# Stick-breaking attention: the scan in place, and a row buffer of its own for the sigmoid

## The chip, the cores and the metric

The kernel runs on one core of one Trainium2 chip. The metric is the device time of one execution in microseconds. Five engines work side by side, each through a list of instructions in a fixed order: TensorE (PE in the profile, its weight loads PEld), VectorE (DVE), ScalarE (ACT), GpSimd (POOL) and SyncE (SP), which issues the DMAs.

## What is computed

One layer of a decoder with 2048 tokens of 1024 channels, all in 32-bit floats. The normalised input is projected to 6144 columns; these feed eight heads of stick-breaking attention and four heads of differential attention, and both branches are gated, merged, projected and normalised again. The change concerns the first branch:

```python
# A[t,s] = beta_ts * prod_{s<j<t}(1-beta_tj), s<t strictly
z = jnp.einsum('bqhd,bkhd->bhqk', q_blk, k) * scale
neg_log_1m_beta = jnp.where(mask, jax.nn.softplus(z), 0.0)
suffix = lax.cumsum(neg_log_1m_beta, axis=3, reverse=True) - neg_log_1m_beta
a = jnp.where(mask, jnp.exp(jax.nn.log_sigmoid(z) - suffix), 0.0)
out = jnp.einsum('bhqk,bkhd->bqhd', a, v)
```

## The kernel before

The sequence is worked off in two halves of 1024 tokens. In each half come four pairs of stick-breaking heads (called heads below, `s00` to `s03` in the first half, `s10` to `s13` in the second), then four differential heads (`d..`), and at the end the output stage (`y`, `o`). While one head attends, the projections of the next head and some of the gate columns are put between its instructions on TensorE (line 177). Their weights arrive by DMA and are split into two parts on GpSimd (lines 136 and 137).

`sb_group` holds the attention of one head for 512 queries. It goes backwards over chunks of 512 keys, from the diagonal chunk (`kc == G`) to chunk 0: one or two chunks in the first half, three or four in the second. A head has two halves of its pair and two groups of queries, so 6 chunks in the first half and 14 in the second. Each chunk has four rows, `r` = 0 to 3, of 128 queries. A row passes through:

- two matmuls for the scores into a PSUM bank (`a_S`, lines 384 and 385; three banks),
- the sigmoid on ACT (line 402), which writes `b`; in the diagonal chunk GpSimd then masks 128 columns of it (line 405),
- `g = 1 - b` on GpSimd (line 406),
- the scan on VectorE (line 408), from the last key to the first: the running product with `g`, less `b`. Each step multiplies the state by `g` and takes `b` from it, so that the state is the running product of `1 - b`, less one. Its start value is the first column of the same row's result in the chunk before. The weights A are the differences of neighbours in this result `R`; the kernel forms these differences on the values instead.

Then `R` is transposed on TensorE in blocks of 128 (line 414, `a_T`, two banks), split into a high and a low part by ACT (line 421, `a_h`) and VectorE (line 422, `a_l`), and multiplied by the values into the accumulator (`a_O`, lines 425 and 426).

`b`, `g` and `R` lie in buffers of the tag `row`: eight of them, each 2 x 512 floats per partition. A row's `b` and `g` share one; the results of two rows share one. So a chunk takes four buffers for `b` and `g` and two for `R`. A `b`/`g` buffer is free when its scan has ended, an `R` buffer when the last transpose of the chunk and the next chunk's scans have read it. The differential heads use the same eight buffers for their rows.

The order on each engine is made when the program is built: a scheduler takes instructions by their place in the code, moved back by fixed offsets for the transposes' products (`LATER_AV`) and the projections (`LATER`), and by `pace_products`, which ties the projections to the score matmuls. It also decides which of the eight buffers a tile gets, and so which earlier reader an instruction has to wait for.

## Time and profile before

| | |
|---|---|
| median of three runs | 2284.68 us (2282.75 to 2286.26) |
| profiled execution, its own time | 2286.18 us |
| its span in the trace | 2284.5 us |
| TensorE (PE) busy | 2184.0 us, 96% |
| VectorE (DVE) busy | 1486.4 us, 65% |
| ScalarE (ACT) busy | 942.7 us, 41% |
| GpSimd (POOL) busy | 846.3 us, 37% |
| scans (line 408, 192 + 128 of the groups shown) | about 385 us of VectorE |
| idle of ACT ahead of the sigmoid, until a scan ended | 202.4 us |
| granted TensorE clock, mean | 0.99 |

The times of one execution stand in a trace of it: one entry for each instruction with engine, line, start and duration, and for each idle stretch the event that ended it. Matmuls overlap, so an engine that is "busy" 96% of the time need not stream 96% of the time. The chain of waits follows the work that ended last back from the end, at each step to what released it.

### The profile page before, as it was taken

Reading aid. Unit: us, or ns where it says so; the run is one execution under the profiler, and the core shown is the slowest. Engines: PE = TensorE matmul, PEld = TensorE weight load, DVE = VectorE, ACT = ScalarE, POOL = GpSimd, SP = SyncE. Lnnn points to the kernel's source line nnn. Section 1 sums busy time; section 2 is a strip of 40 time slices with the busy share of each in tenths; the row PEclk is TensorE's granted clock in tenths of the full one; section 3 lists DMA queues with packets and bytes.
Section 4 is the critical chain, followed back from the end, with each engine's and each line's share of the span. In section 5 each row is a group of like instructions: output and inputs, shape, how many; then the busy total and the mean of one; then the engine's idle time right before and its main releaser. Section 6 shows DMA issues by size and latency. Waiting matters only on the chain.

```text
span 2284.5 us, 33674 instructions
## 1 busy us (share of the span) xinstructions
PE 2184.0 (96%) x11712; PEld 1837.2 (80%) x11712; DVE 1486.4 (65%) x3424; ACT 942.7 (41%) x2004; POOL 846.3 (37%) x1142
## 2 busy tenths in 40 slices
PE   6999999999999999999999999999999998999998
PEld 5788888888888778777777777787888878899997
DVE  6546565467557568787887877777767778444434
ACT  4324344344434434444444445454444444222221
POOL 2546446433232265454544543232222324111110
PEclk9999999999999999999999999999999999999999
DMA  4332323332444221221121121232222424544442
GB/s 127 113 119 93 119 74 109 110 106 84 129 136 132 88 83 56 65 68 62 45 72 51 47 74 53 69 97 66 79 84 75 121 81 158 166 136 143 137 152 90
DMA packets 204890, 220.99 MB, mean 97 GB/s; under 512 B 18864, under 2 KB 149936, under 8 KB 204720
## 3 DMA queue, kind: packets, MB, share of 16 engines
q1 hardware_dynamic: 204720, 218.83, 30.8%
q8 instruction: 93, 1.52, 0.3%
q14 instruction: 77, 0.63, 0.1%
HBM read 134.89 MB, written 67.11 MB: 88 GB/s over the span
## 4 chain that ended last, share of the span: by engine, by line
PE 71%; DVE 12%; ACT 5%; POOL 4%; issue 4%; DMA 3%; SPq 0%; DVEq 0%; ACTq 0%; POOLq 0%
PE g L177 13%; PE o L678 7%; PE y L177 6%; DVE a_R L408 6%; PE f_O L550 4%; PE a_T L414 3%; PE f_S L384 2%; PE zd L177 2%; PE f_S L385 2%; PE f_T L535 2%; POOL a_b L406 2%; PE a_O L425 1%; PE a_S L384 1%; ACT a_b L402 1%; PE a_O L426 1%
## 5 line engine op out<-in xcount | busy, mean ns | idle before, releaser
L406 POOL TENSOR_SCALAR a_b<-a_b 128x512 f32<-128x512 f32 (+2 forms) x320 | 227.1, 714 | 231.4 <-ACT a_b L402 222.6
L408 DVE TENSOR_TENSOR_SCAN a_R<-a_b,a_R 128x512 f32<-128x512 f32 x192 | 261.4, 1368 | 68.8 <-POOL a_b L406 50.9
L402 ACT ACTIVATE a_b<-a_S 128x512 f32<-128x512 f32 (+2 forms) x320 | 166.6, 534 | 244.3 <-DVE a_R L408 202.4
L422 DVE TENSOR_TENSOR a_l<-a_T,a_h 128x512 fp32r<-128x512 f32 (+1 forms) x320 | 186.3, 599 | 83.2 <-ACT a_h L421 72.9
L421 ACT ACTIVATE a_h<-a_T 128x512 fp32r<-128x512 f32 (+1 forms) x320 | 166.3, 534 | 131.7 <-PE a_T L414 112.5
L678 PE MATMUL o<-wt,m 128*128 128x512 f32 x768 | 210.7, 392 | 2.6 <-POOL wt L136 2.1
L514 ACT ACTIVATE f_row<-f_row,f_mx 128x1024 f32<-128x1024 f32 (+4 forms) x192 | 171.2, 894 | 90.4 <-DVE f_mx L507 85.8
L177 PE MATMUL g<-hh,g_w_hi 128*128 128x512 f32 x512 | 202.7, 396 | 0.0
L177 PE MATMUL g<-hl,g_w_hi 128*128 128x512 f32 x512 | 202.6, 396 | 0.0
L177 PE MATMUL g<-hh,g_w_lo 128*128 128x512 f32 x512 | 202.3, 395 | 0.0
L177 PE MATMUL y<-u,woh 128*128 128x256 f32 x1024 | 201.2, 281 | 1.1 <-DMA u<-ul_dram 0.6
L501 DVE CUSTOM_DVE_ANT_0 f_row<-f_S,f_bm 128x512 f32<-128x512 f32 (+3 forms) x304 | 168.6, 572 | 46.7 <-PE f_S L385 27.8
L414 PE MATMUL a_T<-ident,a_R 128*128 128x128 f32 x1088 | 169.7, 274 | 12.8 <-DVE a_l L422 9.4
L414 PEld LDWEIGHTS a_T<-ident,a_R 128*128 128x128 f32 x1088 | 133.2, 141 | 49.5 <-DVE a_l L422 16.8
L177 PEld LDWEIGHTS y<-u,woh 128*128 128x128 f32 x1024 | 165.6, 189 | 6.0 <-DMA u<-ul_dram 1.7
L678 PEld LDWEIGHTS o<-wt,m 128*128 128x128 f32 x768 | 140.4, 188 | 31.2 <-POOL wt L136 2.6
L542 ACT ACTIVATE f_h<-f_T 128x512 fp32r<-128x512 f32 (+2 forms) x176 | 85.2, 495 | 169.9 <-PE f_O L550 93.4
L543 DVE TENSOR_TENSOR f_l<-f_T,f_h 128x512 fp32r<-128x512 f32 (+2 forms) x176 | 98.1, 564 | 83.7 <-ACT f_h L542 80.5
L408 DVE TENSOR_TENSOR_SCAN a_R<-a_b 128x128 f32<-128x128 f32 (+3 forms) x128 | 123.7, 969 | 42.9 <-POOL a_b L406 40.4
L177 PE MATMUL y<-u,wol 128*128 128x256 f32 x512 | 143.0, 280 | 0.0
L136 POOL TENSOR_SCALAR g_w_hi<-g_w_raw 128x512 fp32r<-128x512 f32 x64 | 43.8, 702 | 205.4 <-PE g L177 85.4
L177 PEld LDWEIGHTS g<-hh,g_w_lo 128*128 128x128 f32 x512 | 96.6, 189 | 19.2
(1333 smaller groups left out, 5643.8 us busy)
## 6 DMA issues: line engine op xcount, KB each, us to landing
g_w_raw<-in_w_in_dram SPq DMA_DIRECT2D x64, 256.0 KB, 3.1
g_dram<-g_s SPq DMA_DIRECT2D x64, 256.0 KB, 2.4
x<-in_x_dram SPq DMA_DIRECT2D x16, 512.0 KB, 5.2
u<-uh_dram SPq DMA_DIRECT2D x64, 128.0 KB, 2.9
u<-ul_dram SPq DMA_DIRECT2D x64, 128.0 KB, 3.3
xr<-in_x_dram SPq DMA_DIRECT2D x32, 256.0 KB, 3.4
out_dram<-xr SPq DMA_DIRECT2D x32, 256.0 KB, 2.9
zd_w_raw<-in_w_in_dram SPq DMA_DIRECT2D x16, 256.0 KB, 3.1
```

Of the source, the lines that this page charges most:

```text
L177: pace["fill"].append((nc.tensor.matmul(ps, a[:, c, :], b[c], start=n == 0, stop=n == last).ins, len(pace["att"])))
L402: nc.scalar.activation(b, ps[:, :w], AF.Sigmoid, scale=SCALE)
L406: nc.gpsimd.tensor_scalar(g, b, -1.0, 1.0, ALU.mult, ALU.add)
L408: nc.vector.tensor_tensor_scan(R[r // 2][:, r % 2, :w][:, ::-1], g[:, ::-1], b[:, ::-1], init, ALU.mult, ALU.subtract)
L414: mark("T", nc.tensor.transpose(pt[:, r * P:(r + 1) * P], R[r // 2][:, r % 2, j * P:(j + 1) * P], ident))
L421: nc.scalar.activation(hi[:, c0:], pt[:, c0:], AF.Copy)
L422: nc.vector.tensor_sub(lo[:, c0:], pt[:, c0:], hi[:, c0:].bitcast(F32))
L501: nc.vector.tensor_tensor_reduce(rows[m][(c0 + p0) // HALF][:, (c0 + p0) % HALF:(c0 + p0) % HALF + pw], pss[m][:, p0:p0 + pw], bias_, scal ...
L514: nc.scalar.activation(rows[m][k][:, :w], rows[m][k][:, :w], AF.Exp, bias=mxs[m][:, 7:8], accum_out=sums[k][m])
L543: nc.vector.tensor_sub(lo[:, cs], pt[:, cs], hi[:, cs].bitcast(F32))
L550: mark("O", nc.tensor.matmul(O, a, r[:, ms], start=j == 0 and e == 0, stop=j == i and e == 2))
L678: nc.tensor.matmul(ps, M[a][c][:, tb * P:(tb + 1) * P], wt[m][b][c], start=i == 0, stop=i == 3 * NC - 1)
```

## The change

The two results of a row pair and `g` of the same two rows now lie in one buffer: GpSimd writes `g` into the place of `R`, and the scan overwrites it there. `b` has buffers of its own, one for two rows. A chunk takes two buffers for `b` and two for `R`, all allocated at the head of the chunk.

```diff
--- before.py
+++ after.py
@@ -390,22 +390,22 @@
         O = psO.tile([P, CH], F32, name=f"{n}_O", tag="O")
         prev = None
         for kc in range(G, -1, -1):
-            R = [T([P, 2, CH], F32, f"{n}_R{kc}{k}", "row") for k in range(2)]
+
+            B, R = ([T([P, 2, CH], F32, f"{n}_{x}{kc}{k}", "row") for k in range(2)] for x in "bR")
             for r in range(4):
                 w = P * (r + 1) if kc == G else CH
                 ww = max(w, 256)
                 qs = slice(r * P, (r + 1) * P)
                 ps = psS.tile([P, CH], F32, name=f"{n}_S{kc}{r}", tag="S")
                 qk(ps, K, q, qs, kc * CH, ww)
-                bg_ = T([P, 2, CH], F32, f"{n}_b{kc}{r}", "row")
-                b, g = bg_[:, 0, :w], bg_[:, 1, :w]
+                b, g = (t[r // 2][:, r % 2, :w] for t in (B, R))
                 nc.scalar.activation(b, ps[:, :w], AF.Sigmoid, scale=SCALE)
                 if kc == G:
 
                     nc.gpsimd.affine_select(b[:, qs], b[:, qs], pattern=[[-1, P]], compare_op=ALU.is_gt, fill=0.0, base=0, channel_multiplier=1)
                 nc.gpsimd.tensor_scalar(g, b, -1.0, 1.0, ALU.mult, ALU.add)
                 init = 0.0 if kc == G else prev[r // 2][:, r % 2, 0:1]
-                nc.vector.tensor_tensor_scan(R[r // 2][:, r % 2, :w][:, ::-1], g[:, ::-1], b[:, ::-1], init, ALU.mult, ALU.subtract)
+                nc.vector.tensor_tensor_scan(g[:, ::-1], g[:, ::-1], b[:, ::-1], init, ALU.mult, ALU.subtract)
             prev = R
             for j in range(4):
                 r0 = j if kc == G else 0
```

The instructions are the same in number and shape. What moves is their order and what they wait for. The place shown is one head of the second half (`a1100`, head `s11`), its two full chunks `kc` = 1 and 0. Names end in a chunk and row number and a running number; `b12` is chunk 1, row 2 before the change, while after it `b11` is chunk 1, rows 2 and 3. In brackets stand the engines that an instruction waits for.

ACT before, sigmoids of chunk 1 and the first two of chunk 0, among the high parts of earlier chunks:

```order
L402 ACTIVATE a1100_b11_9951<-a1100_S11_9948 128x512 [waits DVE_49]
L421 ACTIVATE a1011_h11_9658<-a1011_T11_9653 128x512 [waits PE_49]
L402 ACTIVATE a1100_b12_9958<-a1100_S12_9955 128x512 [waits DVE_49,PE_49]
L275 ACTIVATE s12k_a_10023<-s12k_ps1_10128 64x512 [waits PE_49]
L421 ACTIVATE a1011_h12_9669<-a1011_T12_9664 128x512 [waits PE_49]
L421 ACTIVATE a1011_h13_9680<-a1011_T13_9675 128x512 [waits PE_49,Activation_49]
L402 ACTIVATE a1100_b13_9965<-a1100_S13_9962 128x512
L277 ACTIVATE s12k_b_10024<-s12k_ps1_10128 64x512 [waits DVE_49]
L402 ACTIVATE a1100_b00_10059<-a1100_S00_10056 128x512 [waits DVE_49]
L421 ACTIVATE a1011_h00_9768<-a1011_T00_9763 128x512 [waits DVE_49,PE_49]
L402 ACTIVATE a1100_b01_10066<-a1100_S01_10063 128x512 [waits DVE_49]
```

ACT after, the same place:

```order
L402 ACTIVATE a1100_b10_9861<-a1100_S10_9865 128x512
L402 ACTIVATE a1100_b10_9861<-a1100_S11_9871 128x512
L421 ACTIVATE a1011_h10_9573<-a1011_T10_9568 128x512 [waits DVE_49,PE_49]
L421 ACTIVATE a1011_h11_9584<-a1011_T11_9579 128x512 [waits DVE_49,PE_49]
L402 ACTIVATE a1100_b11_9862<-a1100_S12_9877 128x512 [waits DVE_49]
L402 ACTIVATE a1100_b11_9862<-a1100_S13_9883 128x512
L275 ACTIVATE s12k_a_9943<-s12k_ps1_10046 64x512 [waits PE_49]
L421 ACTIVATE a1011_h12_9595<-a1011_T12_9590 128x512 [waits PE_49,Activation_49]
L277 ACTIVATE s12k_b_9944<-s12k_ps1_10046 64x512 [waits DVE_49]
L421 ACTIVATE a1011_h13_9606<-a1011_T13_9601 128x512 [waits PE_49,Activation_49]
L402 ACTIVATE a1100_b00_9974<-a1100_S00_9978 128x512
```

The sigmoids now stand in pairs, and of four one waits for VectorE where three did.

POOL after, `1 - b` of the same two chunks with the split of a weight among them (before, each of them waited for ACT, and none of these but two for another engine):

```order
L406 TENSOR_SCALAR a1100_R10_9863<-a1100_b10_9861 128x512 [waits DVE_49,Activation_49]
L406 TENSOR_SCALAR a1100_R10_9863<-a1100_b10_9861 128x512 [waits Activation_49]
L136 TENSOR_SCALAR zd11_w_hi_10541<-zd11_w_raw0_10543 128x512 [waits DMAHW7_49,PE_49]
L136 TENSOR_SCALAR zd11_w_hi_10541<-zd11_w_raw1_10547 128x512 [waits DMAHW0_49]
L137 TENSOR_TENSOR zd11_w_lo_10542<-zd11_w_raw0_10543,zd11_w_hi_10541 128x512 [waits PE_49,Pool_49]
L137 TENSOR_TENSOR zd11_w_lo_10542<-zd11_w_raw1_10547,zd11_w_hi_10541 128x512 [waits Pool_49]
L406 TENSOR_SCALAR a1100_R11_9864<-a1100_b11_9862 128x512 [waits PE_49,Activation_49]
L406 TENSOR_SCALAR a1100_R11_9864<-a1100_b11_9862 128x512 [waits Activation_49]
L406 TENSOR_SCALAR a1100_R00_9976<-a1100_b00_9974 128x512 [waits DVE_49,Activation_49]
L406 TENSOR_SCALAR a1100_R00_9976<-a1100_b00_9974 128x512 [waits Activation_49]
L406 TENSOR_SCALAR a1100_R01_9977<-a1100_b01_9975 128x512 [waits PE_49,Activation_49]
```

The waits for a buffer that an earlier scan or transpose has to free have moved to the first `1 - b` of each pair.

## Rows read from the trace of the kernel before

**Rows 1.** Busy time by stretch: PE, PEld, DVE, ACT, POOL busy (count); PEclk, DMA, GB/s.

```profile
60.00:445.00 385.00, 382.32 (x1900) 318.67 (x1900) 211.15 (x322) 145.61 (x299) 202.38 (x300) 1.00 0.32 101
806.80:963.80 157.00, 149.84 (x753) 123.36 (x751) 117.28 (x147) 68.58 (x138) 88.48 (x117) 0.99 0.24 74
963.80:1395.00 431.20, 398.04 (x2019) 315.65 (x2018) 341.11 (x407) 204.99 (x404) 222.08 (x306) 0.99 0.19 59
```

**Rows 2.** The same stretches, transposes of line 414 alone: PE, PEld; PEclk, DMA, GB/s.

```profile
60.00:445.00 385.00, 45.11 (x285) 34.90 (x285) 1.00 0.32 101
806.80:963.80 157.00, 25.68 (x168) 20.39 (x167) 0.99 0.24 74
963.80:1395.00 431.20, 93.59 (x602) 73.49 (x601) 0.99 0.19 59
```

**Rows 3.** Chain of waits, full stretch of the first half: start us, us, what.

```profile
344.90 0.77 PE a_T L414 x7
...
346.83 3.44 PE s03q_ps L177 x15
```

**Rows 4.** Waits, TensorE, 60 to 445: us in total, times, longest us.

```profile
PE s00vps L352 <- DVE vcarry L348: 1.5, 1, 1.5
```

**Rows 5.** Waits, all engines, 963.8 to 1395.

```profile
POOL a_b L406 <- ACT a_b L402: 169.0, 92, 3.6
ACT a_b L402 <- DVE a_R L408: 165.4, 99, 4.6
DVE a_R L408 <- POOL a_b L406: 36.8, 51, 1.4
DVE a_l L422 <- ACT a_h L421: 33.5, 38, 1.8
```

**Rows 6.** Chain of waits, 1048 to 1056.

```profile
1048.43 1.63 DVE a_R L408
...
1050.08 0.61 ACT a_b L402
...
1050.76 1.49 POOL a_b L406
...
1052.27 1.30 DVE a_R L408
...
1053.59 0.60 ACT a_b L402
```

**Rows 7.** Timeline, same place: start us, us, engine, line; idle before and releaser.

```profile
1050.55 1.27 DVE L408 TENSOR_TENSOR_SCAN a_R<-a_b,a_R 128x512 f32<-128x512 f32 x1
...
1050.76 1.48 POOL L406 TENSOR_SCALAR a_b<-a_b 128x512 f32<-128x512 f32 x1 [1.78 <-ACT a_b L402]
...
1057.37 0.62 POOL L406 TENSOR_SCALAR a_b<-a_b 128x512 f32<-128x512 f32 x1 [2.48 <-ACT a_b L402]
```

**Rows 8.** Groups of VectorE, 963.8 to 1395: busy us, mean ns, idle us before.

```profile
L408 DVE TENSOR_TENSOR_SCAN a_R<-a_b,a_R 128x512 f32<-128x512 f32 x120 | 162.6, 1358 | 37.4 <-POOL a_b L406 26.8 <-PE a_T L414 7.7 <-POOL g_w_hi L136 1.1
L422 DVE TENSOR_TENSOR a_l<-a_T,a_h 128x512 fp32r<-128x512 f32 (+3 forms) x169 | 102.9, 619 | 34.0 <-ACT a_h L421 33.5
L408 DVE TENSOR_TENSOR_SCAN a_R<-a_b 128x384 f32<-128x384 f32 (+3 forms) x46 | 47.5, 1033 | 11.0 <-POOL a_b L406 10.0
```

**Rows 9.** Tile a_b, 963.8 to 1395: ns min/median/max, first and last start us.

```profile
L406 POOL TENSOR_SCALAR a_b<-a_b x166: 295/620/1514, 964.6 to 1390.0; 128x512 f32<-128x512 f32 x132, 128x384 f32<-128x384 f32 x12, 128x128 f32<-128x128 f32 x11, 128x256 f32<-128x256 f32 x11
L408 DVE TENSOR_TENSOR_SCAN a_R<-a_b,a_R x120: 1252/1284/2293, 968.5 to 1391.0; 128x512 f32<-128x512 f32 x120
L405 POOL TENSOR_SCALAR_AFFINE_SELECT a_b<-a_b x46: 282/293/1220, 964.2 to 1356.6; 128x128 f32<-128x128 f32 x46
```

**Rows 10.** Tile s12k_w_hi, a weight split: ns min/median/max, first and last start us.

```profile
L177 PE MATMUL s12k_ps<-hh,s12k_w_hi x16: 392/397/398, 941.8 to 972.3; 128*128 128x512 f32 x16
...
L137 POOL TENSOR_TENSOR s12k_w_lo<-s12k_w_raw,s12k_w_hi x2: 1298/1300/1303, 928.0 to 929.2; 128x512 fp32r<-128x512 f32 x2
```

**Rows 11.** Group of VectorE, whole span: busy us, mean ns, idle us before.

```profile
L521 DVE SCALAR_TENSOR_TENSOR f_row<-f_row,f_l,f_row 128x512 f32<-128x512 f32 x8 | 6.0, 746 | 0.0
```

## The prediction

> **What bounds the kernel now.** I read the busy time by stretch first [rows 1], then counted what TensorE has to stream in each stretch [rows 1 to 3], then asked who makes it wait [rows 4, 5], and last followed the chain through one of those waits [rows 6, 7]. The changed code runs in two stretches: the stick-breaking heads of the first half of the sequence (60 to 445 us) and those of the second half (807 to 1395 us).
>
> TensorE's busy share does not separate the stages, because pipelined matmuls overlap. What separates them is the time that its instructions need when they stand back to back. A 512-column matmul then takes 3.44/15 = 0.23 us and a 128-column transpose 0.77/7 = 0.11 us [rows 3]; narrower matmuls I scale by columns. By the code each head has 32 matmuls of 256 and 16 of 384 columns. First half, four heads: 1900 instructions, 285 of them transposes [rows 1, 2], so 1423 x 0.23 + 128 x 0.115 + 64 x 0.17 + 285 x 0.11 = 384 us of the 385. TensorE is full there, and its costliest wait in the whole stretch is 1.5 us [rows 4]. Head 0 of the second half: 753 with 168 transposes, so 537 x 0.23 + 32 x 0.115 + 16 x 0.17 + 168 x 0.11 = 148 of 157 us (95%). Heads 1 to 3: 2019 with 602 transposes, so 1273 x 0.23 + 96 x 0.115 + 48 x 0.17 + 602 x 0.11 = 378 of 431 us (88%). **There 53 us are missing**, and only there can this change pay.
>
> What fills the gap: in these 431 us ACT waits 165.4 us, in 99 pieces, ahead of the sigmoid for the scan; POOL waits 169.0 us for the sigmoid; VectorE waits 36.8 us for POOL and 33.5 us for `a_h`, which stands behind the sigmoids on ACT [rows 5]. TensorE takes its part of it from both: a score matmul needs a bank that a sigmoid has emptied, a transpose a finished scan and a bank that `a_l` has left. The chain shows the loop: scan 1.63, sigmoid 0.61, POOL 1.49, scan 1.30, sigmoid, with 0.02 to 0.07 us between them [rows 6]. A sigmoid starts only when the scan of the row before it has ended. This is a buffer, not data: nothing in the mathematics ties row k's sigmoid to row k-1's scan. The eight `row` buffers are mostly held by R tiles that still wait for their transposes, and in the built program one buffer is handed from row to row. One turn without collision is 1.28 + 0.02 + 0.60 + 0.07 + 0.62 + 0.03 = 2.62 us; the stretch gives 431.2/168 rows = 2.57 us. **The loop sets the pace of heads 1 to 3.**
>
> **The change part by part.** No arithmetic is added or removed: 320 sigmoids, 320 `1 - b`, 320 scans as before, with the same shapes.
>
> *Fewer buffers.* A key chunk took six `row` tiles (two R, four b/g); it takes four (two B, two R). The order shows what comes of it: where nearly each sigmoid of a chunk waited on VectorE, only the first of the second pair does, and POOL's first `1 - b` of each pair now waits for VectorE or TensorE instead, since it is the first to write R. By the built program's placement the B pair of rows 2 and 3 takes the buffer of the B pair of rows 0 and 1, the other B pair one that an R gave up; of the R pairs one in two takes the buffer of the B pair just scanned, the other an older R's.
>
> *The new loop*, for four full rows: the scans 4 x 1.284 = 5.14 [rows 9]; ahead of one pair sigmoid, `1 - b` and gaps, 0.60 + 0.62 + 0.14 = 1.36; ahead of the other `1 - b` alone, 0.62 + 0.07 = 0.69; and inside each pair the second `1 - b` meets the first scan. The trace has that meeting: alone the operation took 0.62 us, started 0.2 us after a scan it took 1.48 and ended 0.42 us after it [rows 7], so I add 0.45 twice. Sum 8.09 us, 2.02 a row instead of 2.57, or 3 x 56 x 2.02 = 340 us. VectorE's other work has to find room: `a_l` 102.9 us [rows 8] and some 28 us (341.1 busy [rows 1] less 162.6 + 47.5 + 102.9 [rows 8]). The four `a_l` of a chunk (4 x 0.62 = 2.5 us [rows 8]) fit the 2.95 us of gaps, and the order puts `a_l` and key work between the scan pairs; the 28 us come on top: 368 us. POOL and the scans exclude each other, so their sum bounds too: clean scans 132 x 1.284 + 34 x 0.7 = 193; `1 - b` 132 x 0.62 + 34 x 0.5 = 99; masks 46 x 0.293 = 13 [rows 9]; 15 weights, each two pieces of 1.30 [rows 10] and two of the kind of a `1 - b` (0.62), 58; some 8 for `us_ul` at 1.3. That is 371 us.
>
> So three limits lie close together: VectorE 368, the VectorE and POOL pair 371, TensorE 378. With limits so near none is reached. I take 95% of TensorE's, what head 0 does with the same loop and more matmuls to put into it: 378/0.95 = 398 us, **a gain of 33 us**; the bounds are 0 and 53.
>
> By the Trainium skill (SBUF — State Buffer, "SBUF: two separate sides") the read and write ports that VectorE and GpSimd share are an exclusive lock for a whole instruction, held by a VectorE operation with two SBUF inputs against a GpSimd one that reads SBUF. By that rule the blocked `1 - b` ends its whole 0.62 us after the scan, 0.65 with the gap stands twice in the loop, and a row takes (8.09 + 0.40)/4 = 2.12 us, 357 for the three heads instead of 340. The trace agrees that the two exclude each other, but with 0.42 after the scan [rows 7], so that I keep 0.45; under either TensorE's 378 comes first.
>
> *Head 0* loses 157 - 148 = 9 us, in part at the turn between the halves; I take 2 of the 9. *First half*: nothing to gain at 384 of 385 us. *Scan in place*: the nearest row that overwrites an input is the 128x512 of `f_row`, 0.746 us [rows 11], against 0.62 for a mean `a_l` [rows 8]; at most 0.13 us a scan, 21 us over 168 rows on an engine with 90 us idle (431.2 - 341.1), so 0 on the path. *Moved instructions elsewhere*: the scheduler renumbers everything, but the differential heads and the output stage keep their buffers: 0, with 3 us either way. *Wait added on POOL*: behind it stand the weight splits, which the projections need. The trace has them early: `s12k_w_lo` ended at 930.5 and its first matmul began at 941.8 [rows 10], so 11 us cover it.
>
> Sum: 33 + 2 = 35 us. The profiled execution took 2286.18 us (span 2284.5), 1.5 above the median of the runs; 2286.2 - 35 = 2251, less 1.5: **2250 us**.
>
> **Rivals.** *The limits collide more* (gain 8 to 20, 2265 to 2277): scans in pairs, with POOL held under each, leave `a_l` late and TensorE's transposes wait. For it: 368, 371 and 378 are near each other, and the scans already average 1.358 us against 1.284 clean [rows 8, 9]. Against: the new loop's gaps match the `a_l` almost exactly. *TensorE reaches its limit* (378 us as in the first half: gain 53 + 5, 2227). Against: there VectorE is busy 211 of 385 us, here it would be 341 of 378 [rows 1]. *The change doesn't do what it says* (2280 to 2289): the freed buffers are swallowed by R tiles, which now are taken at `1 - b` instead of at the scan, about 2 us earlier, and wait for the same transposes; sigmoids then still go one by one. Against: the placement and the order's waits. *Slower*: POOL's `1 - b` waits for transposes of a chunk that TensorE has queued behind projections whose weights are still to be split on POOL. A block decides from 11.3 us; a chunk lasts 431.2/42 = 10.3 us, so a buffer that comes two chunks late (20.5) makes a projection 9.2 us late. Four such among the 15 weights eat 37 us, the whole gain; eight give 74 - 35 = 39 us more than before, 2323. For it: POOL works in order, and a wait for the buffer of R now stands on it. Against: those R tiles were transposed chunks earlier in the order.
>
> **How the numbers follow.** Forecast, 2237 to 2265: 0.60. Limits collide, 2265 to 2280: 0.16. TensorE's limit, below 2237: 0.08. No effect: 0.06. Slower: 0.10. The range leaves out the last two and a tip at either end: 2232 to 2277. What a measurement of this kernel can tell from no change is about 0.2%, 4.6 us: faster 0.84, within 0.06, slower 0.10.
>
> **What would show it.** Right: heads 1 to 3 take about 398 us instead of 431; ACT's wait for the scan ahead of the sigmoid falls from 165 us to under 60, VectorE's for `1 - b` from 37 to under 20; the first half stays at 385. POOL gains waits for VectorE and TensorE that cost nobody. Wrong in its size: VectorE over 90% busy there and TensorE still at 88 to 91%. Wrong in kind: projections that wait for weight splits, scans longer than 1.284 us where POOL is idle, or a first half beyond 390 us.

## The result

The change makes the kernel slower: 2338.53 us (median of four runs, 2333.7 to 2341.84) against 2284.1 of the kernel before on the same chip, ratio 1.0236 with the interval 1.0214 to 1.0257. The prediction was 2250.

The profiled execution has a span of 2332.0 us, 47.5 more than before. In the first half I take the start of a head as its first score matmul; in the second half as its first score against keys of the first half (tiles `s10k` to `s13k` and `d10k`), which in the stick-breaking heads comes 7 to 16 us behind the scores of the diagonal chunk. Starts are rounded, so the differences hold to 1 us. Counted so, the heads took (us):

| | before | after |
|---|---|---|
| four stick-breaking heads, first half | 394 | 398 |
| differential heads, first half | 369 | 369 |
| `s10` | 157 | 156 |
| `s11`, `s12`, `s13` | 143, 146, 134 (422 in all) | 156, 159, 144 (459) |
| first differential head, second half | 124 | 134 |
| the rest | 817 | 816 |

Counted from the first score of all, heads 1 to 3 took 433 us before and 467 after, `s10` 155 and 157. The loss lies in heads 1 to 3 of the second half, where the gain was expected, and ten more stand in the differential head behind them, in which their last chunks end. Engines and groups of the page after, with busy time, share and count, and for a group the mean in ns and the idle time ahead of it:

```profile
PE 2193.9 (94%) x11712; PEld 1841.5 (79%) x11712; DVE 1492.7 (64%) x3424; ACT 939.7 (40%) x2004; POOL 834.7 (36%) x1142
...
L408 DVE TENSOR_TENSOR_SCAN a_R<-a_R,a_R,a_b 128x512 f32<-128x512 f32 x192 | 272.3, 1444 | 35.0 <-POOL a_R L406 34.6
L406 POOL TENSOR_SCALAR a_R<-a_b 128x512 f32<-128x512 f32 (+2 forms) x320 | 202.9, 648 | 252.7 <-PE a_T L414 117.7
...
L402 ACT ACTIVATE a_b<-a_S 128x512 f32<-128x512 f32 (+2 forms) x320 | 157.1, 535 | 208.7 <-DVE a_R L408 150.7
```

No engine has much more to do. GpSimd's `1 - b` even got shorter (mean 648 ns, 714 before), and its idle time ahead of that line now ends with TensorE: 117.7 us wait for a transpose. By stretch (as [rows 1]; the last row is heads 1 to 3):

```profile
60.00:445.00 385.00, 378.35 (x1878) 314.98 (x1877) 207.50 (x311) 143.49 (x293) 208.94 (x294) 1.00 0.31 99
809.00:965.00 156.00, 148.21 (x728) 121.23 (x727) 112.65 (x138) 65.28 (x132) 83.80 (x109) 0.98 0.25 75
965.00:1424.00 459.00, 400.37 (x1983) 315.91 (x1982) 337.66 (x402) 197.46 (x396) 196.31 (x303) 0.98 0.17 53
```

The same heads before, 422 us of the 431 of [rows 1]:

```profile
964.00:1386.00 422.00, 389.04 (x1970) 308.40 (x1969) 333.33 (x399) 200.68 (x397) 215.63 (x299) 0.99 0.19 59
```

TensorE stands idle 59 us of the stretch, 33 before (its length less PE busy), and is busy 11 us longer, of which the granted clock explains up to 7 (last section). VectorE is busy 338 us (333 before), in a stretch that is 37 us longer: 74% instead of 79%. The waits in heads 1 to 3 after (us in total, times, longest), to be held against [rows 5]:

```profile
ACT a_b L402 <- DVE a_R L408: 113.0, 36, 5.5
POOL a_R L406 <- PE a_T L414: 102.2, 16, 9.8
ACT a_h L421 <- PE a_T L414: 82.2, 46, 4.3
POOL a_R L406 <- DVE a_R L408: 75.6, 34, 3.1
DVE a_l L422 <- ACT a_h L421: 70.0, 48, 4.1
...
PE a_S L384 <- ACT a_b L402: 35.5, 29, 2.5
DVE a_R L408 <- POOL a_R L406: 28.9, 48, 2.2
```

and of the same 422 us before:

```profile
ACT a_b L402 <- DVE a_R L408: 162.8, 98, 4.6
...
ACT a_h L421 <- PE a_T L414: 28.0, 31, 1.7
...
PE a_S L384 <- ACT a_b L402: 19.5, 26, 2.1
```

ACT's wait for the scan fell from 163 to 113 us, in 36 pieces instead of 98, so longer ones. New is the second line: sixteen times, 6.4 us on average, GpSimd stands before a `1 - b` until TensorE has transposed an old R. ACT's wait for transposes grew from 28 to 82 us, VectorE's for `a_h` from 32 to 70, TensorE's for the sigmoid from 20 to 36.

One of the sixteen, in order. In TensorE's order of the built program stand (names with their numbers; lines between left out)

```
L384 MATMUL a1111_S22_10886<-s11k_b_8512,s11q_1_1_1_9778 128x512
...
L384 MATMUL a1111_S23_10892<-s11k_b_8512,s11q_1_1_1_9778 128x512
...
L177 MATMUL s13k_ps0_11377<-hh_1_0_7857,s13k_w_hi_11365 128x512
...
L414 MATMUL a1110_T12_10631<-ident_78,a1110_R10_10583 128x128 x2
...
L414 MATMUL a1110_T13_10642<-ident_78,a1110_R11_10584 128x128 x2
```

`S22` and `S23` are the scores of rows 2 and 3 of a chunk. The results of both, `a1111_R21`, take the buffer of `a1110_R10`, whose last transposes (in `T12` and `T13`) come behind twelve projection matmuls of `s13k`. TensorE on the chip:

```profile
1084.91 0.39 PE L384 MATMUL a_S<-s11k_b,s11q 128*128 128x512 f32 x1
...
1088.61 0.39 PE L384 MATMUL a_S<-s11k_b,s11q 128*128 128x512 f32 x1
...
1096.35 0.40 PE L177 MATMUL s13k_ps<-hh,s13k_w_hi 128*128 128x512 f32 x1
...
1099.11 1.04 PE L414 MATMUL a_T<-ident,a_R 128*128 128x128 f32 x8
```

and the other engines (idle time before an instruction and what ended it in brackets):

```profile
1092.61 1.09 ACT L402 ACTIVATE a_b<-a_S 128x512 f32<-128x512 f32 x2 [1.81 <-DVE a_R L408]
...
1100.09 1.20 POOL L406 TENSOR_SCALAR a_R<-a_b 128x512 f32<-128x512 f32 x2 [9.81 <-PE a_T L414]
...
1100.45 0.69 DVE L422 TENSOR_TENSOR a_l<-a_T,a_h 128x512 fp32r<-128x512 f32 x1 [4.09 <-ACT a_h L421]
1101.06 1.30 DVE L408 TENSOR_TENSOR_SCAN a_R<-a_R,a_R,a_b 128x512 f32<-128x512 f32 x1
```

The two sigmoids had written b by 1093.7. Their `1 - b` could start only at 1100.09, when the transposes had read the old R; VectorE had nothing for 4.09 us and then got two scans at once. TensorE itself hardly paused here: it worked off projections that nobody waited for, ahead of transposes that everybody waited for. It pays later, when scores need banks that sigmoids have not emptied.

### The profile page after: what moved, and what is told of

It reads as the page before. It is cut to its first block, busy times and chain, and to the rows that moved or that the text cites. A ratio compares the mean times of both kernels' runs of the same rounds, so it can differ in the third digit from the quotient of the medians.

```text
span 2332.0 us, 33651 instructions
## 1 busy us (share of the span) xinstructions
PE 2193.9 (94%) x11712; PEld 1841.5 (79%) x11712; DVE 1492.7 (64%) x3424; ACT 939.7 (40%) x2004; POOL 834.7 (36%) x1142
## 5 line engine op out<-in xcount | busy, mean ns | idle before, releaser
L408 DVE TENSOR_TENSOR_SCAN a_R<-a_R,a_R,a_b 128x512 f32<-128x512 f32 x192 | 272.3, 1444 | 35.0 <-POOL a_R L406 34.6
L406 POOL TENSOR_SCALAR a_R<-a_b 128x512 f32<-128x512 f32 (+2 forms) x320 | 202.9, 648 | 252.7 <-PE a_T L414 117.7
L402 ACT ACTIVATE a_b<-a_S 128x512 f32<-128x512 f32 (+2 forms) x320 | 157.1, 535 | 208.7 <-DVE a_R L408 150.7
L408 DVE TENSOR_TENSOR_SCAN a_R<-a_R,a_b 128x128 f32<-128x128 f32 (+3 forms) x128 | 110.5, 883 | 35.8 <-POOL a_R L406 33.1
```

What stands on the lines that cost most here:

```text
L402: nc.scalar.activation(b, ps[:, :w], AF.Sigmoid, scale=SCALE)
L406: nc.gpsimd.tensor_scalar(g, b, -1.0, 1.0, ALU.mult, ALU.add)
L408: nc.vector.tensor_tensor_scan(g[:, ::-1], g[:, ::-1], b[:, ::-1], init, ALU.mult, ALU.subtract)
```

## The experiments

Two measures are used below, for heads 1 to 3 of the second half. Their time, counted as in the table above, is read from the traces. **Lead** is read from the built program: the TensorE work (0.23 us for 512 columns, 0.11 for a transpose, as [rows 3]) by which the first score of a row pair (for `b`, of its row) stands ahead of the last transpose that reads the old R in the buffer that this R or `b` takes, a mean over the tiles that take an R's buffer. In the example it reaches from `S22` to `T13`.

I began with two theories. **A**: `1 - b` takes R some 2 us earlier than the scan did, and so waits for transposes. **B**: buffers of `b` are released by pairs, after two scans, so sigmoids go in pairs and the three score banks run dry.

**Pairs without the scan in place.** `b` and `g` in pairs, R a buffer of its own, taken by the scan.

```diff
-            B, R = ([T([P, 2, CH], F32, f"{n}_{x}{kc}{k}", "row") for k in range(2)] for x in "bR")
+            B, Gt, R = ([T([P, 2, CH], F32, f"{n}_{x}{kc}{k}", "row") for k in range(2)] for x in "bgR")
```

> b and g each get buffers for two rows, but the scan writes into R buffers of its own: six tiles a chunk as before, in pairs, and R is claimed by the scan and not by 1 - b. Theory A (the change is slow because 1 - b now claims R and so stands behind the transposes that free it): R is claimed late again, the time falls back to within 15 us of before, 2270 to 2300, and POOL's wait for TensorE ahead of line 406 falls from 118 us to under 30. Theory B (the change is slow because b is freed for two rows at once, after two scans): as slow as the change or slower, 2325 to 2360, with ACT's wait for the scan at 110 us or more in heads 1 to 3.

2333.02 us (ratio 1.0222, 1.0199 to 1.0244): as slow as the change, without the early R. Against A.

**In place with a `b` for each row.** R is taken early as in the change, `b` as before.

```diff
-                b, g = (t[r // 2][:, r % 2, :w] for t in (B, R))
+                b, g = T([P, 2, CH], F32, f"{n}_b{kc}{r}", "row")[:, 0, :w], R[r // 2][:, r % 2, :w]
```

> The scan writes over 1 - b in place, but b has a buffer for each row (half of it unused), so b is freed after one scan. Theory A: slower than before all the same, since 1 - b still claims R: 2315 to 2360, with POOL waiting for TensorE ahead of line 406 for over 80 us. Theory B: back at before, 2275 to 2295, and POOL waits for TensorE under 30 us.

2302.03 us (1.0086, 1.0071 to 1.0101), heads 1 to 3 427 us: nearer to B's range than to A's, and 7 us above it. Some 20 of the 54 us stay with the early R; most goes with the pairs. It looked like B.

**A ninth buffer**, for the change and for the kernel before, with the memory taken from `Tl` and `zs`. That slows the end of the run by some 64 us in both (from the start of the last differential head 575 and 572 us against 510), so the four heads are what is read.

```diff
-    BUFS = {"K": 6, "V": 6, "Q": 8, "row": 8, "Th": 2, "Tl": 3, "vt": 1, "dv": 1, "zs": 2, "u": 2, "bm": 1, "bd": 1}
+    BUFS = {"K": 6, "V": 6, "Q": 8, "row": 9, "Th": 2, "Tl": 2, "vt": 1, "dv": 1, "zs": 1, "u": 2, "bm": 1, "bd": 1}
```

> The change with nine row buffers in place of eight; the room comes from one zs and one Tl buffer less. By the placement R then takes the buffer of an R from 4 chunks before instead of 3, while b pairs are still handed on inside a chunk. Theory A: the loop through TensorE's transposes is broken, POOL's wait for TensorE ahead of line 406 falls under 30 us, heads 1 to 3 fall from 467 us to 400 to 425, and the whole to 2255 to 2290 unless the two lost buffers cost more. Theory B: the b pairs are handed on as in the change, so 2325 to 2345.

> Control: the kernel before with the same nine row buffers and the same two buffers less. Theory A: its b/g buffer is still handed from row to row, so the loop of scan, sigmoid and 1 - b stays: 2275 to 2290. Theory B: the same, since it has no pairs. If the lost zs and Tl buffers cost much, it shows here: over 2290.

The change took 2411.69 us (1.0567, 1.0551 to 1.0583), the kernel before 2341.95 (1.0266, 1.0249 to 1.0283). The four heads of the change went from 615 to 637 us, those of before from 579 to 573. GpSimd's wait for transposes in the change did not shrink:

```profile
POOL a_R L406 <- PE a_T L414: 135.0, 22, 8.9
```

It was 102.2 in 16. The scheduler spent the buffer on running scores further ahead: in TensorE's built order the first transpose of a chunk now stands 31 us of work behind the chunk's last score instead of 27. The Trainium skill (Perfetto Trace Analysis, "Optimization Strategy") says that a gap which repeats on the engine that should be saturated can mean too little SBUF for the next tile. The trace has such gaps on TensorE, 59 us in heads 1 to 3 of the change, but with one buffer more they were larger, 71 us of 481.

**`b` kept for a head pair.** The change's eight buffers; the two of `b` are taken once and written again row by row, so that a row's half is free after its own scan (the last line stands in `sb_attend`; its passing on is left out).

```diff
-            B, R = ([T([P, 2, CH], F32, f"{n}_{x}{kc}{k}", "row") for k in range(2)] for x in "bR")
+            R = [T([P, 2, CH], F32, f"{n}_R{kc}{k}", "row") for k in range(2)]
+        B = [T([P, 2, CH], F32, f"b{hf}{p}{k}", "row") for k in range(2)]
```

> The change, but the two b buffers of a head pair are taken once for the whole head pair and written again chunk after chunk, instead of being taken anew for each chunk. The same eight buffers, the scan in place and R taken at 1 - b as in the change; what differs is the release: a row's half of b is free as soon as that row's own scan of the chunk before has read it, not when both scans of the pair have. Theory B (the pair's release makes sigmoids go in pairs, the score banks run dry and everything on TensorE behind them is bunched): the four heads of the second half fall from 615 us to 570 to 592, as in the kernel before (579), the run takes 2270 to 2300. Theory A (1 - b takes R early and waits for transposes, which is still so here): they stay at 605 to 625 us, the run at 2325 to 2350.

2339.59 us (1.0244, 1.0225 to 1.0263), the four heads 615 us. These are A's numbers, but A stands against the run without the scan in place. B falls: the release by pairs is gone, ACT waits 108 times for short scans instead of 36 times, and nothing is gained.

```profile
POOL a_R L406 <- PE a_T L414: 125.5, 24, 10.6
ACT b L402 <- DVE a_R L408: 115.8, 108, 3.5
```

**The same on the kernel before**, with four `b`/`g` buffers kept (taken in `sb_attend`) and so four for R.

```diff
-                bg_ = T([P, 2, CH], F32, f"{n}_b{kc}{r}", "row")
+                bg_ = BG[r]
+        BG = [T([P, 2, CH], F32, f"b{hf}{p}{k}", "row") for k in range(4)]
```

> The kernel before, with four b/g buffers taken once for a head pair, each written again by the same row of the next chunk, and so four left for R, two chunks deep. R is taken at the scan as before. Theory B: no sigmoid waits for the scan of the row ahead of it any more, ACT's wait for the scan in heads 1 to 3 of the second half falls from 163 us to under 60, and the run takes 2255 to 2285. A third theory, C (what counts is how far TensorE's transposes may stay behind the scores: R buffers that hold three chunks are needed): scans wait for transposes, the four heads take over 600 us instead of 579, the run 2300 to 2345. Theory A has nothing against this kernel and gives 2255 to 2285 as well.

2337.87 us (1.024, 1.0223 to 1.0257). The kernel before, with R taken late and no row waiting for the row ahead of it, is as slow as the change, which is against A. It is what theory C of this expectation had given. But with `b` kept above R had six buffers, three chunks deep, and that kernel was as slow, so the depth alone isn't it. ACT's wait for the scan halved, and scans now wait for transposes:

```profile
ACT b L402 <- DVE a_R L408: 83.2, 110, 1.8
...
DVE a_R L408 <- PE a_T L414: 34.8, 26, 3.9
```

**`1 - b` on ACT.** The kernel before without GpSimd in the loop, but for the mask of `g` in the diagonal chunk, whose two lines are left out here.

```diff
-                nc.gpsimd.tensor_scalar(g, b, -1.0, 1.0, ALU.mult, ALU.add)
+                nc.scalar.activation(g, ps[:, :w], AF.Sigmoid, scale=-SCALE)
```

> The kernel before, with 1 - b made on ACT as the sigmoid of the negated score instead of on POOL, so that a row needs two ACT instructions and its scan meets no 1 - b on VectorE's port (the masked block of a diagonal row is set on POOL for both). If the row-to-row loop through one b/g buffer sets the pace, a turn is 1.28 + 0.60 + 0.60 + 0.07 = 2.55 us against 2.57 measured: no change, 2272 to 2295. If the meeting of scan and 1 - b is what costs (scans mean 1.358 us against 1.284 clean, and 1 - b up to 1.48 instead of 0.62), heads 1 to 3 gain 12 to 30 us: 2250 to 2272. If ACT, with 0.6 us more for each of 320 rows, becomes the bound somewhere: above 2295.

2285.92 us (1.0004, 0.9995 to 1.0014). Without the meeting of scan and `1 - b` nothing is gained, unless ACT's added 0.60 us a row ate it, which this run cannot tell. Of the loop it says nothing, since the loop with ACT in GpSimd's place gave the same time. The exclusive port that the Trainium skill states (SBUF — State Buffer, "SBUF: two separate sides") agrees in kind with the 1.48 us of a blocked `1 - b` [rows 7]; that one ended 0.42 us after the scan, though, where the rule leaves it its whole 0.62.

What the slow kernels had in common was TensorE's order: the scores stood in clumps (15 to 19 spaces over 4 us between two scores, 3 to 9 in the quick ones). Theory **D**: the order costs. So I changed the order, and in the code nothing else; the scheduler then hands the eight buffers out anew.

**The change and the kernel before, scores tied to transposes.** In the second half the score of row r may not stand ahead of the transposes j = r of the chunk three before. The tie sets the order when the program is built; on the chip it adds no wait. `lastT` collects the last transpose of each bank `j` (lines between left out). In the views of these kernels the added lines move the sigmoid to line 406, `1 - b` to 410, the scan to 412 and the transposes to 418.

```diff
+                lastT.append(tr.ins)
-                qk(ps, K, q, qs, kc * CH, ww)
+                first = qk(ps, K, q, qs, kc * CH, ww)
+                if hf and len(lastT) >= 12:
+                    tc.add_manual_dep(first, lastT[r - 12].name, mybir.DependencyInfo(mybir.DependencyClass.NoSync, mybir.DependencyReason.DATA), reason="even")
```

> The change, with an order added for TensorE in the second half and nothing else: the score of row r of a chunk stands behind the transposes j = r of the chunk three before. In the built program the scores are then spaced evenly: the standard deviation of the TensorE work between one score and the next falls from 1.14 us (before: 0.89; the slow variants so far 1.14 to 1.39, the quick ones 0.78 to 1.01), and of 160 spaces over 4 us there are 3 instead of 15. Buffers, release by pairs and R taken at 1 - b are those of the change. Theory D (the new buffers let the scheduler place scores, fill and transposes in clumps on TensorE, and this order, not the waits for buffers themselves, is what costs): the four heads of the second half fall from 615 us to 565 to 592, the run to 2245 to 2305. Theories A and B (the waits for R, or the release of b by pairs): 600 to 625 us, 2320 to 2345.

> The kernel before with the same order added on TensorE (score of row r behind the transposes j = r of the chunk three before), the spread of the spaces falls from 0.89 to 0.55 us. Theory D: the four heads take 560 to 578 us instead of 579, the run 2260 to 2284. A and B say nothing of it: no change, 2278 to 2292. If the loop scan, sigmoid, 1 - b, scan through one b buffer sets the pace here, whatever TensorE's order is, no change either, and this kernel is then slower than the change with the same order.

The change: 2295.34 us (1.0044, 1.0027 to 1.0061), 43 of the 54 us are back, and GpSimd's and ACT's waits with them:

```profile
980.00:1387.00 407.00, 381.87 (x1965) 311.06 (x1965) 326.21 (x396) 207.51 (x395) 208.53 (x293) 0.98 0.19 59
```

```profile
POOL a_R L410 <- PE a_T L418: 41.4, 14, 4.5
ACT a_b L406 <- DVE a_R L412: 39.5, 24, 2.9
```

The kernel before: 2274.53 us (0.9947, 0.9932 to 0.9962), half a per cent faster than it was:

```profile
958.00:1366.00 408.00, 383.95 (x1965) 310.32 (x1963) 332.98 (x397) 204.97 (x395) 230.69 (x295) 0.97 0.19 59
```

```profile
ACT a_b L406 <- DVE a_R L412: 110.6, 93, 2.6
```

With the same order heads 1 to 3 take 407 and 408 us with either set of buffers (from the first score of all 422 and 418). TensorE's wait for the sigmoid, 35.5 us in the change and 19.5 before, is among the waits of neither. TensorE now stands idle 25 and 24 us, so in the change this wait is what came back. And the quicker kernel before still has 110 us of ACT's wait for the scan: that wait was not what held it.

**Two chunks back** instead of three (`lastT[r - 8]`), on the change and on the kernel before.

> The change with the score of row r behind the transposes j = r of the chunk two before instead of three: the same even spaces (0.56 us), but in TensorE's stream the first transpose of a chunk comes 10.6 us after its last score instead of 19.5 (26.7 in the change without the order). Theory D with no more to it (evenness alone counts): as with three chunks. If the lag has to cover sigmoids, four scans in a row and the fill: transposes wait for scans, the four heads take over 600 us, the run 2310 to 2360.

> The kernel before with the score of row r behind the transposes j = r of the chunk two before, so that the order leaves R and b 2.8 us behind the transposes that free them, instead of 1.8 ahead for R with three chunks. Theory E, with distance as the only cost: as with three chunks or up to 6 us better, 2266 to 2279. If the shorter lag between a chunk's scores and its transposes (10.6 us of TensorE work instead of 19.5) begins to cost: 2280 to 2310.

2279.69 us (0.9967, 0.9955 to 0.9979) and 2272.61 (0.9949, 0.9934 to 0.9963); heads 1 to 3 407 us in both. The change with an order is 0.3% faster than the kernel before without one. It gains 16 us on the tie of three, which evenness alone does not give; by this count they lie outside heads 1 to 3, from the first score of all 7 of them inside. In the kernel before ACT's wait for the scan is down to 1.0 us in 2 pieces, and heads 1 to 3 take the time that they take with 110.6 us of it.

**One kept `b` buffer**, written by rows in turn, seven buffers for R, no tie (the lines that take `B[0]` and R are left out).

```diff
-                b, g = (t[r // 2][:, r % 2, :w] for t in (B, R))
+                b, g = B[0][:, r % 2, :w], R[r // 2][:, r % 2, :w]
```

> The variant in which b is kept for a head pair, with one buffer for it instead of two: rows write its halves in turn, so that a sigmoid waits for the scan two rows before, and R has seven buffers. Few rows are in flight, as in the kernel before, but the scores stand as unevenly in TensorE's order as in the change (1.20 us, 13 spaces over 4 us). Theory D: as slow as the change, the four heads 605 to 625 us, the run 2325 to 2350. If what costs is that four rows' sigmoids may run ahead: 575 to 592 us, 2280 to 2305.

2290.02 us (1.0018, 1.0009 to 1.0028), heads 1 to 3 416 us, in spite of clumps as in the change. So clumps are not the cause, and D in that form falls. The other reading, that rows in flight cost, fits this run; but the change with the tie has as many in flight as the change without, and takes 407. The waits for transposes are half of those of the two-buffer variant:

```profile
ACT b L402 <- DVE a_R L408: 139.1, 135, 3.1
POOL a_R L406 <- PE a_T L414: 62.5, 21, 5.1
```

What did agree in the main with the times of all kernels was the lead. Theory **E**: scores that stand far ahead of the transposes that must free their buffers cost.

**Clumps without a lead.** The change with all four scores of a chunk behind the last transpose of the chunk three before (`lastT[-9]`).

> The change, with the order on TensorE that all four scores of a chunk stand behind the last transpose of the chunk three before. The scores then come in clumps (the spread of the spaces between them is 1.91 us, 42 are over 4 us; the change has 1.14 and 15), but none stands ahead of a transpose that frees the buffer of its row (1.5 us behind it on average; in the change 9.1 us ahead for R and 5.9 for b). Theory D (clumps cost): the four heads of the second half take 615 us or more, the run 2330 to 2380. Theory E (the distance costs): 570 to 597 us, 2285 to 2312.

**A lead in between**: the kernel before with two kept `b`/`g` buffers (`BG[r % 2]`), no tie.

> The kernel before with two b/g buffers kept for a head pair and written by rows in turn, six buffers for R, which is taken at the scan. Clumps as in the change (1.12 us, 16 spaces over 4 us); the scores stand 7.5 us of TensorE work ahead of the transposes that free their R, between 6.2 of before and 9.1 of the change. Theory D: the four heads take 605 to 625 us, the run 2320 to 2345. Theory E: 583 to 603 us, 2290 to 2318.

2291.27 us (1.0033, 1.002 to 1.0046), the four heads 583 us, and 2300.89 (1.0068, 1.0051 to 1.0085), 595 us. Both as E said and D did not. In the clumped kernel GpSimd waits for sigmoids, and its wait for transposes is not among the waits any more:

```profile
979.00:1396.00 417.00, 385.85 (x1963) 315.92 (x1962) 337.65 (x395) 206.54 (x393) 219.26 (x294) 0.96 0.19 58
```

```profile
POOL a_R L410 <- ACT a_b L406: 120.6, 46, 4.2
```

**One kept `b` buffer with the tie**, three chunks back, two, and three in both halves.

> The variant with one kept b buffer written by rows in turn, with the score of row r behind the transposes j = r of the chunk three before: R stands 0.9 us behind the transposes that free it instead of 5.8 ahead. Theory E: the four heads 560 to 568 us instead of 570, s11 to s13 405 to 410 as in the other kernels with the order, the run 2276 to 2288. If what quickened this variant is the small number of rows in flight and not the distance, the order changes nothing: 2286 to 2294.

> The kept b buffer with the score of row r behind the transposes j = r of the chunk two before: R stands 9.9 us of TensorE work behind the transposes that free it, instead of 0.9 with three chunks. Theory E says that only a score ahead of those transposes costs: the four heads 550 to 562 us (554 with three chunks), the run 2266 to 2280. If the lag of 10.6 us from a chunk's last score to its first transpose is short for scans on a VectorE that is over 80% busy: the four heads 565 to 575 us as with the change's own buffers, 2280 to 2292.

> The kept b buffer with the order three chunks back in both halves. In the first half the four heads took 401 us in the variant with the order in the second half alone, 394 in the kernel before. If those 7 us come of the order of scores and transposes: 392 to 397 us there, the run 2264 to 2272. If they come of something else (the other engines' queues, projections): 399 to 405, the run 2270 to 2278.

2272.88 us (0.9948, 0.9933 to 0.9963), 2280.26 (0.9973, 0.9964 to 0.9983) and 2272.46 (0.9943, 0.9928 to 0.9958). The first has the quickest heads 1 to 3 of all, 396 us, better than expected, so that few rows in flight are not all that quickened this variant; TensorE stands idle 16 us there:

```profile
970.00:1366.00 396.00, 379.82 (x1962) 310.85 (x1961) 323.90 (x397) 208.19 (x394) 211.21 (x295) 0.98 0.19 61
```

```profile
ACT b L406 <- DVE a_R L412: 24.5, 22, 2.3
```

Two chunks back it is slower (408), as I had expected of the short distance from a chunk's scores to its transposes. No run isolates that, and neither the change nor the kernel before lost by it. In both halves the tie gains nothing in the first, 401 us as without it.

All kernels, by lead (negative: the score stands behind the transposes; "-": `b` takes no R's buffer; brackets: with the slower end). The medians come from several chips, on which the kernel before took 2282.4 to 2286.5 us:

| kernel | lead of R, b (us) | s10 to s13 | s11 to s13 | median us |
|---|---|---|---|---|
| before, 4 b/g kept | 13.5, - | 613 | 445 | 2337.9 |
| change, b kept | 11.2, - | 615 | 455 | 2339.6 |
| pairs, not in place | 9.7, 6.0 | 622 | 464 | 2333.0 |
| **change** | 9.1, 5.9 | 615 | 459 | 2338.5 |
| change, nine buffers | 9.0, 6.4 | 637 | 481 | (2411.7) |
| before, 2 b/g kept | 7.5, - | 595 | 433 | 2300.9 |
| before, nine buffers | 6.3, 4.0 | 573 | 422 | (2342.0) |
| **before** | 6.2, 4.2 | 579 | 422 | 2284.1 |
| in place, b per row | 6.1, 4.4 | 591 | 427 | 2302.0 |
| before, 1 - b on ACT | 6.0, 4.5 | 580 | 425 | 2285.9 |
| one b kept | 5.8, - | 570 | 416 | 2290.0 |
| before, tie 3 | 1.8, -0.3 | 563 | 408 | 2274.5 |
| change, tie 3 | 1.7, -2.3 | 573 | 407 | 2295.3 |
| one b kept, tie 3 | -0.9, - | 554 | 396 | 2272.9 |
| change, clumps | -1.5, -1.8 | 583 | 417 | 2291.3 |
| before, tie 2 | -2.8, -2.9 | 569 | 407 | 2272.6 |
| change, tie 2 | -3.0, -6.7 | 567 | 407 | 2279.7 |
| one b kept, tie 2 | -9.9, - | 568 | 408 | 2280.3 |

Every kernel with 9 us or more takes 613 to 637 us for the four heads, every one with at most 6.3 takes 554 to 591. It is no law: among the slow ones more lead is not slower, below zero nothing more is gained, and the kernel with a `b` per row and the kernel before differ by 12 us at the same lead.

## Why the prediction was wrong

**The step that failed** is in "Fewer buffers" and "The new loop". It noted that half of the R pairs take "an older R's" buffer and that a `b` pair takes "one that an R gave up", and priced both at nothing: 0.69 us ahead of the second scan pair, 8.09 a chunk. The trace after has 16 such waits of 6.4 us, 102.2 us. The loop that I closed over scan, sigmoid and `1 - b` leads in truth through TensorE's order: score, `b`, `1 - b` into an old R's place, and that R's transposes, which stand behind the score. I had read that R was transposed "chunks earlier in the order". For the order of the change this is wrong: on average 9.1 us of TensorE's work stands between, and a row whose R takes such a buffer cannot be quicker than that. It was wrong for the kernel before as well (6.2 us).

**"The loop sets the pace of heads 1 to 3"** was wrong for the kernel before as well. The loop is not closed on every row: in the built order 78 of the 168 rows take the `b` and `g` buffer of the row just before, 38 that of two rows before and 48 an old R's. With TensorE's order tied, the heads of this kernel take 408 us, 2.43 a row by the count that gives 2.51 before, and less than the loop's 2.62. So it was chance that 2.62 us a turn came so near to the measured 2.57 a row. A wait that fills an engine's idle time (ACT's 165 us) says who came last, not that taking it away brings the time back: with the tie of two chunks it is 1.0 us, with that of three 110.6, and the heads take the same.

**Why fewer buffers per chunk made the lead larger.** With a `b` handed on row by row the scheduler could place a score only when the scan of a row before had gone, which kept scores back. With four rows of `b` in flight, in pairs or kept, it places them as soon as it can, and the transposes as late as the buffers allow. That the order is the cause is shown by the ties. That the lead is what counts in it rests on the two kernels that were forecast by it and on the table, with the exceptions named there. That the freed buffers are what moved the lead is argued from the built orders (without a tie, four rows in flight: 9 to 13.5 us; one or two: 5.8 to 7.5) and not tested by itself.

**The rival "slower"** named the right instruction, GpSimd's `1 - b` that waits for queued transposes, but the wrong victim, and had 10% of the chance. The weight splits come in good time: `s13k`'s low part was ready at 1080.2, its first product began at 1096.3 (as [rows 10] before), and in the four heads TensorE waits for weight splits once, 1.1 us for a weight load, as before:

```profile
L177 PE MATMUL s13k_ps<-hh,s13k_w_hi x16: 388/395/628, 1096.3 to 1137.5; 128*128 128x512 f32 x16
...
L137 POOL TENSOR_TENSOR s13k_w_lo<-s13k_w_raw,s13k_w_hi x2: 1297/1303/1309, 1077.6 to 1078.9; 128x512 fp32r<-128x512 f32 x2
```

The victims were the scans, which came late and in bursts, and through sigmoids and banks TensorE's scores.

**Head 0**: 156 us after 157, from its first score of all 157 after 155; 2 less were expected. **The first half**: expected without change, it lost 4 us. TensorE waits there for `a_l` where it did not before; this is TensorE's one wait of over 2 us in all:

```profile
PE a_O L426 <- DVE a_l L422: 5.2, 3, 1.7
```

The tie in both halves was run on the kept `b` buffer alone, whose first half took 401 us with it and without. Between the two kernels with the tie of three 21 us remain: 6 in the first half, 4 in its differential heads and 10 in `s10` (166 and 156 us; from the first score of all 5 in `s10` and 4 in heads 1 to 3). That part stays open.

**The scan in place** costs next to nothing, as said. Its fastest and median time in heads 1 to 3 were 1252 and 1284 ns [rows 9], and now

```profile
L408 DVE TENSOR_TENSOR_SCAN a_R<-a_R,a_R,a_b x117: 1251/1303/2249, 965.4 to 1423.3; 128x512 f32<-128x512 f32 x117
```

that is 2 us over 117 scans. The page's mean is 1444 ns instead of 1368, 15 us over the 192 scans of that group, on an engine that now stands idle more than before.

**The signs that I had named**: ACT's wait for the scan fell to 113 us, not under 60, VectorE's for `1 - b` from 37 to 29, not under 20, and GpSimd's new waits for TensorE and VectorE, which were to "cost nobody", are 102.2 and 75.6 us. Of the signs of being wrong none came: VectorE is at 74%, no projection waits for a split for longer than that 1.1 us.

**What was right**: TensorE's missing 53 us could be had in part. Heads 1 to 3 fell from 422 to 407 us with an order alone and to 396 with an order and one kept `b` buffer. The prediction counted to the last head's end, 431 us where this count has 422; so 396 is some 405 in its terms, against the 398 that it expected of the change. Its sum for TensorE took the 24 transposes of lines 352 and 467 in these heads for 512-column products, which makes 378 some 3 us too much and changes nothing here.

## What to carry to other kernels

When a change alters which buffer is handed to whom, look in the built order of the engine that works in order for the distance between the first instruction that needs the buffer and the last that frees it; work that stands between can become a wait, and another buffer need not shorten it. Try an order tie early: here it was worth more (12 us faster than before, 43 of 54 us for the change) than any rearrangement of buffers without one. Do not take an engine's largest wait for the bound because a loop through it adds up to the right time; take the loop apart in a run.

## What the runs showed of the hardware

A short pause of TensorE cost twice here. At the start of `s11` after the change it stood still for some 2 us, for a sigmoid, and then streamed 512 columns every 0.43 us instead of every 0.23:

```profile
966.25 0.40 PE L177 MATMUL s12k_ps<-hh,s12k_w_hi 128*128 128x512 f32 x1
966.48 0.40 PE L177 MATMUL s12k_ps<-hl,s12k_w_hi 128*128 128x512 f32 x1
...
970.88 0.72 PE L384 MATMUL a_S<-s11k,s11q 128*128 128x512 f32 x1 [2.22 <-ACT a_b L402]
971.39 0.63 PE L385 MATMUL a_S<-s11k,s11q 128*128 128x512 f32 x1
971.82 0.63 PE L177 MATMUL s12k_ps<-hh,s12k_w_lo 128*128 128x512 f32 x1
```

The granted clock in steps of 2 us (the last three numbers are clock, DMA share and GB/s):

```profile
969.00:971.00 2.00, 0.12 (x1) 0.12 (x2) 1.21 (x3) 0.67 (x2) 0.41 (x2) 1.00 0.02 4
971.00:973.00 2.00, 2.00 (x5) 1.61 (x6) 1.36 (x2) 1.30 (x3) 0.48 (x2) 0.50 0.00 0
973.00:975.00 2.00, 2.00 (x7) 1.52 (x7) 0.02 (x1) 0.00 (x0) 0.00 (x0) 0.65 0.00 0
```

0.50 is the lower of its two levels, 1.2 GHz. In the four heads I count three such falls before (at 819, 983 and 1129 us) and eight after (the first at 823, the last at 1233), which by the granted clock cost 5.1 and 13.7 us of full speed: up to 9 of the 36 us. They follow from the waits and do not explain them: the clumped kernel lost 14 us more to its falls than before in heads 1 to 3 and was still quicker there than the kernel before.
